# Packed attention and conditioning products held together, heads formed earlier, and an output projection over all columns at once, in a two-layer diffusion backbone

## The chip, the cores and the metric

The kernel runs on one core of one Trainium2 chip. The metric is the device time of one execution in microseconds (us). The engines are PE (TensorE, matrix products; PEld is its weight load), DVE (VectorE), ACT (ScalarE), POOL (GpSimd) and SP (SyncE, which here only issues transfers). Each engine works through its own list of instructions in order.

## The reference

Two layers over 256 context tokens and 256 latent tokens of width 1024. Each layer is an adaptive RMS norm, one input projection into three head groups (differential attention, multi-head latent attention, a two-directional gated recurrence), one output projection with a gated residual, and then the same around a squared-ReLU MLP. The shifts, scales and gates come from a conditioning vector and `w_mod`. Cut to what matters here:

```python
for l in range(2):
    mod = split(silu(c) @ w_mod[l] + b_mod[l], 6)          # 6 x 1024 columns, for latent and for context
    pl, pc = project(ada_norm(x, ...)), project(ada_norm(xc, ...))
    # differential attention (6 heads): softmax of two score sets, P0 - lam * P1, times v
    o_da  = diff_attn_core(pl['da_q'], k_da, v_da, lam)
    # latent attention (6 heads): scores of q_nope and q_rope against k_nope and k_rope, softmax, times v
    o_mla = mla_core(pl['q_nope'], pl['q_rope'], kn_all, kr_all, v_all)
    y = concat([da_post(o_da), o_mla, hgrn2_out(...)])     # 1024 wide
    x = x + mod[2] * (y @ w_out[l])
    x = x + mod[5] * (square(relu(ada_norm(x) @ w_ff1[l])) @ w_ff2[l])
    # in layer 0 the context tokens go the same way
return rmsnorm(x, g_final)
```

## The kernel before, in words

Activations are kept with features on the partitions. A float32 product in the large projections is made of three products of two rounded parts (`mm3`, L139 to L142: high by high, low by high, high by low). Weights come in units of 128 x 1024 through four `raw` buffers; ACT copies a unit into its high part `wh` and DVE subtracts to get the low part `wl` (`wunit`, L135 and L136), or POOL does, for as many units as the list `low` holds.

The program is written as one stream. A scheduler puts it into an order for each engine, by the priority of the place in the stream and by when it holds operands to be there; instructions that depend on nothing of each other can so be pulled apart.

Attention walks over steps: a differential step and a latent step in turn, one query tile of 128 rows each, three pairs of heads, 48 steps in layer 0 (four query tiles) and 24 in layer 1 (two). Each step has a part A (scores on PE, L930 and L1225; maximum on DVE; exponential on ACT), two steps later a part B (transposes of the probabilities, L907, and a copy out to `PT` or `mPT`), and a latent step has, three steps later, a part C for itself and its differential mate: the products of the probabilities with the values (L1239). The latent step's product writes one half of the output's 128 partitions and its mate's the other (`tile_position`), two or four key tiles each. A latent head's query and key (`mla_head`) are made by nine products, two ACT copies, a DVE shuffle and three POOL operations (L1191 to L1193); it is formed while its predecessor's step `nq // 2` is at hand. The steps of the next differential pair are staged by six small transfers on SP's queue and six on POOL's (L888).

Between steps of layer 0 a filler (`mod_group`) makes 4096 of the conditioning columns: two groups, each of eight sets, one for each eighth of the input. A set loads two `raw` units (L389, 512 KB each) and makes four products with a stationary operand of 32 columns (L392), one for each quarter of the output's partitions.

At the end of a layer's attention stand `late` tasks, among them the last pair's norm (`da_post`: L956 and a chain of small DVE operations) and the turning of the results into `yh` and `yl` (`turn_y`: L898, L901, L967 to L974). The output projection `proj_out` takes 512 columns at a time: in layer 1, six input tiles in three units for each half, and two more input tiles beside the steps. Each finished column tile is added to the residual on DVE (`ev_res`, L1011), squared on ACT and summed on DVE (L266) for the next norm, whose inputs `mhh` and `mhl` (L306, L307) the MLP's first product reads.

Of the kernel before, what the change touches and what calls it, by code (L numbers as in the profile page):

```python
# [8 lines left out]
F32 = mybir.dt.float32  # L9
# [31 lines left out]
def net(ctx: ExitStack, tc, x, c, cx, c_ctx, w_mod, b_mod, g_mix, g_mlp, w_in, w_out, da_lambda, da_subln_g,  # L41
# [97 lines left out]
    def mm3(ps, lh, ll, rh, rl, start, stop):  # L139
        PE.matmul(ps, lh, rh, start=start, stop=False)  # L140
        PE.matmul(ps, lh, rl, start=False, stop=False)  # L141
        PE.matmul(ps, ll, rh, start=False, stop=stop)  # L142

# [237 lines left out]

    def mod_group(l, g):
        started.append(1)
        ps = psum("mm")
        for k in range(KT):
            for hf in range(2):
                raw = raw_tile()
                c0 = g * 2048 + hf * 1024
                nc.sync.dma_start(out=raw, in_=w_mod[l].rearrange("(p k) f -> p k f", k=KT)[:, k, c0:c0 + 1024])  # L389
                for q in range(2):  # L390
                    j = 2 * hf + q
                    PE.matmul(ps[32 * j:32 * j + 32, :], scm[:, k, :], raw[:, 512 * q:512 * q + 512],  # L392
                              start=(k == 0), stop=(k == KT - 1))
            yield
# [197 lines left out]
    def layer(l):  # L592
# [432 lines left out]


# [184 lines left out]
        def mla_step(p, h, qi, qt, res):  # L1211
# [21 lines left out]
            def C():  # L1233
                d = s.mate
                op = psum("sc")
                for j in range(nk):
                    js = slice(128 * j, 128 * j + 128)
                    for PT, v, c, r in ((d.PT, dav, 2 * p + 1 - h, 1 - h), (s.PT, mv, hd, h)):
                        PE.matmul(op[64 * r:64 * r + 64, 0:128], v[:, j, 64 * c:64 * c + 64], PT[:, js], start=(j == 0),  # L1239
                                  stop=(j == nk - 1), tile_position=(0, 64 * r))  # L1240
                for r, o in ((1 - h, d.res["o"]), (h, res["o"])):
                    S.copy(out=o[64 * r:64 * r + 64, q0:q0 + 128], in_=op[64 * r:64 * r + 64, 0:128])
# [4 lines left out]
        def mla_steps():  # L1247
            order = [1, 0, 3, 2, 5, 4]
            for p in range(3):
                res = {}  # L1250
                for h in (1, 0):
                    for qi, qt in enumerate(qtiles):
                        s = mla_step(p, h, qi, qt, res)
                        n = 2 * p + 1 - h
                        if qi == nq // 2 and n < 5:
                            s.after = lambda n=n: heads.update({order[n + 1]: mla_head(order[n + 1], n + 1)})
# [17 lines left out]
        final = proj_out(0, 6 if last else KT, 512, True)  # L1274
# [21 lines left out]
        for _ in range(2):  # L1296
            step(final)
        if last:
            low.extend([G] * 3)
# [8 lines left out]
        with tc.tile_pool(name=f"mlp{l}", bufs=1) as fp:  # L1308
            fp.tile([128, 920], F32, name="gap")
# [135 lines left out]
```

## Time and profile before

| what | value |
|---|---|
| three runs: median (lowest to highest) | 1233.94 us (1233.19 to 1235.56) |
| the profiled execution: its time, its span | 1233.96 us, 1232.1 us |
| mean granted clock of PE | 0.993 |
| busy: PE, PEld, DVE, ACT, POOL | 1192.5, 964.9, 886.3, 581.8, 111.4 us |
| chain that ended last, by engine | PE 85%, DVE 8%, ACT 3%, POOL 1%, issue 1%, DMA 1% |
| moved by DMA | 170.93 MB, mean 139 GB/s |

The time of an execution is its span and a little around it. Busy time is the time in which an engine had at least one instruction at work; instructions on PE overlap, so that the mean length of one is more than the step from one to the next. The chain is followed back from the last instruction, at each step to what released it.

### The profile page before, as it was taken

Reading aid. Unit: us, or ns where it says so; the run is one execution under the profiler, and the core shown is the slowest. Engines: PE = TensorE matmul, PEld = TensorE weight load, DVE = VectorE, ACT = ScalarE, POOL = GpSimd, SP = SyncE. Lnnn points to the kernel's source line nnn. Section 1 sums busy time; section 2 is a strip of 40 time slices with the busy share of each in tenths; the row PEclk is TensorE's granted clock in tenths of the full one; section 3 lists DMA queues with packets and bytes.
Section 4 is the critical chain, followed back from the end, with each engine's and each line's share of the span. In section 5 each row is a group of like instructions: output and inputs, shape, how many; then the busy total and the mean of one; then the engine's idle time right before and its main releaser. Section 6 shows DMA issues by size and latency. Waiting matters only on the chain.

```text
span 1232.1 us, 21466 instructions
## 1 busy us (share of the span) xinstructions
PE 1192.5 (97%) x8318; PEld 964.9 (78%) x8318; DVE 886.3 (72%) x1786; ACT 581.8 (47%) x1114; POOL 111.4 (9%) x156
## 2 busy tenths in 40 slices
PE   6999999999999999999999999999998998999997
PEld 4677888855568777878787877787986678999997
DVE  4676587767676998765778675896788868765864
ACT  3534444576664553211233332554347874644653
POOL 2200000222200100000000000230003421000000
PEclk9999999999999999999999999999999998999999
DMA  9632223456543346555555555143314404555562
GB/s 325 191 85 57 69 58 100 120 155 196 184 168 103 103 136 194 189 165 162 177 156 156 170 170 151 55 122 92 93 54 131 127 18 135 176 186 178 184 186 69
DMA packets 138199, 170.93 MB, mean 139 GB/s; under 512 B 10883, under 2 KB 116033, under 8 KB 138097
## 3 DMA queue, kind: packets, MB, share of 16 engines
q1 hardware_dynamic: 134816, 164.08, 44.1%
q0 software_dynamic: 2704, 4.94, 1.7%
q8 instruction: 66, 1.08, 0.4%
q10 hardware_dynamic: 576, 0.53, 0.1%
q14 instruction: 37, 0.30, 0.1%
HBM read 160.21 MB, written 1.05 MB: 131 GB/s over the span
## 4 chain that ended last, share of the span: by engine, by line
PE 85%; DVE 8%; ACT 3%; POOL 1%; issue 1%; DMA 1%; SPq 0%; POOLq 0%; ACTq 0%; DVEq 0%
PE mm L140 21%; PE mm L142 21%; PE mm L141 20%; PE sc L1239 3%; PE sc L1225 2%; PE mm L392 2%; PE tp L907 2%; PE mm L218 2%; PE mm L219 2%; PE mm L220 2%; DVE wl L136 1%; PE sc L797 1%; PE mm L930 1%; PE sc L768 1%; PE sc L691 1%
## 5 line engine op out<-in xcount | busy, mean ns | idle before, releaser
L135 ACT CAST wh<-raw 128x1024 fp32r<-128x1024 f32 (+2 forms) x204 | 210.7, 1034 | 278.3 <-PE mm L141 199.6
L136 DVE TENSOR_TENSOR wl<-raw,wh 128x1024 fp32r<-128x1024 f32 (+2 forms) x201 | 242.6, 1209 | 108.8 <-ACT wh L135 106.3
L140 PE MATMUL mm<-mhh,wh 128*128 128x512 f32 (+1 forms) x512 | 173.0, 338 | 0.9 <-DVE fz L336 0.9
L140 PE MATMUL mm<-fa,wh 128*128 128x512 f32 (+1 forms) x512 | 172.5, 337 | 0.0
L141 PE MATMUL mm<-fb,wh 128*128 128x512 f32 (+1 forms) x512 | 171.9, 336 | 0.0
L142 PE MATMUL mm<-fa,wl 128*128 128x512 f32 (+1 forms) x512 | 171.9, 336 | 0.0
L142 PE MATMUL mm<-mhh,wl 128*128 128x512 f32 (+1 forms) x512 | 171.4, 336 | 0.4 <-DVE wl L136 0.4
L141 PE MATMUL mm<-mhl,wh 128*128 128x512 f32 (+1 forms) x512 | 171.7, 335 | 0.0
L426 DVE SCALAR_TENSOR_TENSOR room<-raw,scm,room 128x1024 f32<-128x1024 f32 x84 | 106.4, 1287 | 57.1 <-DMA raw<-in_w_mod_dram 57.1
L140 PE MATMUL mm<-hh,wh 128*128 128x512 f32 (+1 forms) x336 | 126.5, 381 | 4.6 <-ACT hh L351 3.3
L141 PE MATMUL mm<-hl,wh 128*128 128x512 f32 (+1 forms) x336 | 127.0, 378 | 2.3 <-DVE hl L352 2.3
L142 PE MATMUL mm<-hh,wl 128*128 128x512 f32 (+1 forms) x336 | 126.6, 377 | 1.1 <-DVE wl L136 1.1
L140 PEld LDWEIGHTS mm<-mhh,wh 128*128 128x128 f32 x512 | 96.3, 188 | 14.1 <-ACT wh L135 1.7
L140 PEld LDWEIGHTS mm<-fa,wh 128*128 128x128 f32 x512 | 97.0, 190 | 12.4 <-ACT wh L135 1.7
L142 PEld LDWEIGHTS mm<-fa,wl 128*128 128x128 f32 x512 | 97.1, 190 | 10.1
L141 PEld LDWEIGHTS mm<-fb,wh 128*128 128x128 f32 x512 | 97.2, 190 | 9.9
L142 PEld LDWEIGHTS mm<-mhh,wl 128*128 128x128 f32 x512 | 96.3, 188 | 11.0 <-DVE wl L136 0.8
L141 PEld LDWEIGHTS mm<-mhl,wh 128*128 128x128 f32 x512 | 96.3, 188 | 9.6
L140 PEld LDWEIGHTS mm<-hh,wh 128*128 128x128 f32 x336 | 63.4, 190 | 15.7 <-ACT hh L351 4.1
L141 PEld LDWEIGHTS mm<-hl,wh 128*128 128x128 f32 x336 | 64.2, 191 | 13.8 <-DVE hl L352 4.0
L142 PEld LDWEIGHTS mm<-hh,wl 128*128 128x128 f32 x336 | 64.1, 191 | 13.2 <-DVE wl L136 2.0
L347 POOL TENSOR_TENSOR nt<-nt,bc 128x256 f32<-128x256 f32 x24 | 27.0, 1131 | 483.6 <-ACT bc L326 436.1
(333 smaller groups left out, 2189.6 us busy)
## 6 DMA issues: line engine op xcount, KB each, us to landing
raw<-in_w_ff_dram SPq DMA_DIRECT2D x128, 512.0 KB, 3.8
raw<-in_w_mod_dram SPq DMA_DIRECT2D x80, 512.0 KB, 3.8
raw<-in_w_in_dram SPq DMA_DIRECT2D x42, 512.0 KB, 3.8
mraw<-in_w_mod_dram SPq DMA_DIRECT2D x32, 256.0 KB, 6.1
raw<-in_w_out_dram SPq DMA_DIRECT2D x10, 512.0 KB, 3.8
raw<-in_w_in_dram SPq DMA_DIRECT2D x16, 256.0 KB, 5.3
raw<-in_w_in_dram SPq DMA_DIRECT2D x8, 384.0 KB, 3.2
K<-dah POOLq DMA_DIRECT2D x48, 64.0 KB, 2.4
```

Of the source, the lines that this page charges most:

```text
L135: S.copy(out=wh, in_=raw)
L136: (low.pop() if low else V).tensor_sub(out=wl, in0=raw, in1=wh.bitcast(F32))
L140: PE.matmul(ps, lh, rh, start=start, stop=False)
L141: PE.matmul(ps, lh, rl, start=False, stop=False)
L142: PE.matmul(ps, ll, rh, start=False, stop=stop)
L218: PE.matmul(ps, a, wh[:, k, 0:w], start=st, stop=False)
L219: PE.matmul(ps, a, wl[:, k, 0:w], start=False, stop=False)
L220: PE.matmul(ps, b, wh[:, k, 0:w], start=False, stop=sp)
L347: G.tensor_mul(out=ts, in0=ts, in1=self.bc[:, a - T0:b - T0])
L392: PE.matmul(ps[32 * j:32 * j + 32, :], scm[:, k, :], raw[:, 512 * q:512 * q + 512], start=(k == 0), stop=(k == KT - 1))
L426: V.scalar_tensor_tensor(out=acc[r], in0=raw, scalar=scm[:, k, r:r + 1], in1=acc[r], op0=ALU.mult, op1=ALU.add)
L1239: PE.matmul(op[64 * r:64 * r + 64, 0:128], v[:, j, 64 * c:64 * c + 64], PT[:, js], start=(j == 0), stop=(j == nk - 1), tile_position=(0, 6 ...
```

## The change

It has six parts. First, `in_line` ties instructions in the order of a list, without a wait. Part C of a latent step ties its products, the latent one ahead of its mate's for each key tile, and gives them a high priority. Second, `mod_group` does the same with the four products of a set, and loads a set one call of the filler ahead of its products. Third, in layer 1 a head is formed at its predecessor's first step. Fourth, in layer 1 the last output projection takes one input tile and all 1024 columns at a time (`proj_wide`), in four PSUM tiles of two column tiles each; four input tiles of six go ahead of the `late` tasks (before: the first four input tiles for half of the columns). Fifth, `low` holds two units then, where it held three. Sixth, the tile `gap` is left out in layer 1.

```diff
     def mm3(ps, lh, ll, rh, rl, start, stop):
-        PE.matmul(ps, lh, rh, start=start, stop=False)
+        first = PE.matmul(ps, lh, rh, start=start, stop=False)
         PE.matmul(ps, lh, rl, start=False, stop=False)
         PE.matmul(ps, ll, rh, start=False, stop=stop)
+        return first
...
+    def in_line(instrs):
+
+        for a, b in zip(instrs, instrs[1:]):
+            tc.add_manual_dep(b.ins, a.ins.name, mybir.DependencyInfo(mybir.DependencyClass.NoSync,
+                                                                     mybir.DependencyReason.DATA), reason="in line")
+
     def mod_group(l, g):
         started.append(1)
         ps = psum("mm")
+
+        def load(k):
+            raws = [raw_tile() for _ in range(2)]
+            for hf in range(2):
+                c0 = g * 2048 + hf * 1024
+                nc.sync.dma_start(out=raws[hf], in_=w_mod[l].rearrange("(p k) f -> p k f", k=KT)[:, k, c0:c0 + 1024])
+            return raws
+
+        raws = load(0)
+        yield
         for k in range(KT):
-            for hf in range(2):
-                raw = raw_tile()
-                c0 = g * 2048 + hf * 1024
-                nc.sync.dma_start(out=raw, in_=w_mod[l].rearrange("(p k) f -> p k f", k=KT)[:, k, c0:c0 + 1024])
-                for q in range(2):
-                    j = 2 * hf + q
-                    PE.matmul(ps[32 * j:32 * j + 32, :], scm[:, k, :], raw[:, 512 * q:512 * q + 512],
-                              start=(k == 0), stop=(k == KT - 1))
+            now, raws = raws, load(k + 1) if k < KT - 1 else None
+            with tc.high_priority(1000):
+                in_line([PE.matmul(ps[32 * j:32 * j + 32, :], scm[:, k, :], now[j // 2][:, 512 * (j % 2):512 * (j % 2) + 512],
+                                   start=(k == 0), stop=(k == KT - 1)) for j in (2, 3, 0, 1)])
             yield
...
+        def proj_wide(ks):
+
+
+            pss = [psum("mm") for _ in range(4)]
+            ev = ev_res(16, 0, True)
+            for n, k in enumerate(ks):
+                wh, wl = wunit(w_out[l], 0, (k,), [(0, DM)])
+                yh, yl = (ydst[x][:, k, T0q:] for x in "hl")
+                for i in range(KT):
+                    ps, cs = pss[i // 2][:, 256 * (i % 2):256 * (i % 2) + 256], slice(128 * i, 128 * i + 128)
+                    first = mm3(ps, wh[:, 0, cs], wl[:, 0, cs], yh, yl, n == 0 and i % 2 == 0,
+                                n == len(ks) - 1 and i % 2 == 1)
+                    if n == 0 and i % 2:
+                        in_line([clear, first])
+                    clear = first
+                    if n == len(ks) - 1 and i % 2:
+                        ev(i - 1, pss[i // 2][:, 0:256])
+                        ev(i, ps)
+                yield
...
-                for j in range(nk):
-                    js = slice(128 * j, 128 * j + 128)
-                    for PT, v, c, r in ((d.PT, dav, 2 * p + 1 - h, 1 - h), (s.PT, mv, hd, h)):
-                        PE.matmul(op[64 * r:64 * r + 64, 0:128], v[:, j, 64 * c:64 * c + 64], PT[:, js], start=(j == 0),
-                                  stop=(j == nk - 1), tile_position=(0, 64 * r))
+                with tc.high_priority(1000):
+                    in_line([PE.matmul(op[64 * r:64 * r + 64, 0:128], v[:, j, 64 * c:64 * c + 64], PT[:, 128 * j:128 * j + 128],
+                                       start=(j == 0), stop=(j == nk - 1), tile_position=(0, 64 * r))
+                             for j in range(nk) for PT, v, c, r in ((s.PT, mv, hd, h), (d.PT, dav, 2 * p + 1 - h, 1 - h))])
...
-                        if qi == nq // 2 and n < 5:
+                        if qi == (0 if last else nq // 2) and n < 5:
...
-        final = proj_out(0, 6 if last else KT, 512, True)
+        final = proj_wide((0, 1, 3, 4, 5, 2)) if last else proj_out(0, KT, 512, True)
...
-        for _ in range(2):
+        for _ in range(4 if last else 2):
             step(final)
         if last:
-            low.extend([G] * 3)
+            low.extend([G] * 2)
...
-            fp.tile([128, 920], F32, name="gap")
+            if not last:
+                fp.tile([128, 920], F32, name="gap")
```

The order that the scheduler makes of it, at three places. The changed kernel's lines have other numbers: L1239 becomes L1270, L392 becomes L405, L907 becomes L920, L930 becomes L943, L1225 becomes L1258, L970 to L974 become L983 to L987, L1011 becomes L1024, and L266 and L307 become L267 and L308.

PE, some ten steps into layer 0's attention, before (`PT` are a differential step's probabilities, `mPT` a latent step's):

```order
L930 MATMUL mm<-K_2489,Q_2488 128x256 x2
L1239 MATMUL sc<-PT,dav 64x128
L392 MATMUL mm<-raw,scm 32x512
L907 MATMUL tp<-ident,P_2628 128x128 x2
L1239 MATMUL sc<-mPT,mv 64x128
L1239 MATMUL sc<-PT,dav 64x128
L1239 MATMUL sc<-mPT,mv 64x128
L1239 MATMUL sc<-PT,dav 64x128
L1239 MATMUL sc<-mPT,mv 64x128
L1239 MATMUL sc<-PT,dav 64x128
L1239 MATMUL sc<-mPT,mv 64x128
L392 MATMUL mm<-raw,scm 32x512
```

and at about the same place now:

```order
L141 MATMUL mm<-ckl,ukh 64x512
L1270 MATMUL sc<-mPT,mv 64x128
L1270 MATMUL sc<-PT,dav 64x128
L1270 MATMUL sc<-mPT,mv 64x128
L1270 MATMUL sc<-PT,dav 64x128
L405 MATMUL mm<-raw,scm 32x512 x4
L920 MATMUL tp<-ident,P_2627 128x128 x2
L920 MATMUL tp<-ident,mP 128x128 x2
L1258 MATMUL sc<-mk_2635,mq 128x512
```

A step's products and a set's four products stand together now, where one product of a step stood alone, with conditioning products before and after the rest. Over all of layer 0 the 64 conditioning products stand in 27 pieces before and 19 now (one row of eight counts as two), the attention products of 24 steps in 34 runs before and 25 now; in layer 1 those of 12 steps in 22 before and 12 now.

ACT, at the end of layer 1's attention, before (`oda` and `om` are the two kinds of attention's results):

```order
L1242 COPY oda<-sc 64x128
L1242 COPY om<-sc 64x128
L953 ACTIVATE P<-oda 128x256
L135 CAST wh<-raw 128x1024 x2
L970 CAST yh<-om 128x256
L292 CAST mhh<-modT_122 128x8x2
L973 ACTIVATE yh<-oda,vT_91 128x256
```

and now:

```order
L1274 COPY oda<-sc 64x128
L1274 COPY om<-sc 64x128
L966 ACTIVATE P<-oda 128x256
L135 CAST wh<-raw 128x1024 x4
L983 CAST yh<-om 128x256
L293 CAST mhh<-modT_122 128x8x2
L986 ACTIVATE yh<-oda,vT_91 128x256
```

Four weight casts stand ahead of the latent result's `yh` now, two before; the fourth is that of the MLP's first unit. On PE, 26 projection products stood before between the last sums of squares (L956) and the last transposes (L901, four in a row), and 72 stand there now (L969 and L914).

DVE, from the first residual addition of the tail on, before:

```order
L1011 SCALAR_TENSOR_TENSOR xT<-mm,modT_122,xT 128x256 x4
L136 TENSOR_TENSOR wl<-raw,wh 128x1024
L266 TENSOR_TENSOR nsq<-nsq 128x256
L307 SCALAR_TENSOR_TENSOR mhl<-xT,Gm_124,mhh 128x256
```

and now:

```order
L1024 SCALAR_TENSOR_TENSOR xT<-mm,modT_122,xT 128x256 x4
L267 TENSOR_TENSOR nsq<-nsq 128x256
L1024 SCALAR_TENSOR_TENSOR xT<-mm,modT_122,xT 128x256
L267 TENSOR_TENSOR nsq<-nsq 128x256
L1024 SCALAR_TENSOR_TENSOR xT<-mm,modT_122,xT 128x256
L267 TENSOR_TENSOR nsq<-nsq 128x256
L1024 SCALAR_TENSOR_TENSOR xT<-mm,modT_122,xT 128x256
L267 TENSOR_TENSOR nsq<-nsq 128x256
L1024 SCALAR_TENSOR_TENSOR xT<-mm,modT_122,xT 128x256
L308 SCALAR_TENSOR_TENSOR mhl<-xT,Gm_124,mhh 128x256
```

The first input of the norm (`mhl`) stood behind four additions, a weight subtraction and a sum; now it stands behind all eight additions and four sums.

## Rows read from the trace of the kernel before

**Rows 1.** The page: span, and busy us of PE with its share of the span.

```profile
span 1232.1 us, 21466 instructions
...
PE 1192.5 (97%) x8318; PEld 964.9 (78%) x8318; DVE 886.3 (72%) x1786; ACT 581.8 (47%) x1114; POOL 111.4 (9%) x156
```

**Rows 2.** Stretches: us; busy us (instructions) of PE, PEld, DVE, ACT, POOL; granted clock; DMA.

```profile
252.00:368.00 116.00, 115.86 (x754) 65.67 (x753) 81.93 (x230) 75.29 (x222) 22.43 (x39) 1.00 0.60 183
943.50:990.00 46.50, 41.72 (x280) 28.66 (x278) 39.53 (x95) 40.17 (x103) 22.89 (x39) 1.00 0.39 109
990.00:1013.67 23.67, 23.67 (x189) 17.29 (x188) 15.49 (x47) 17.20 (x47) 4.56 (x4) 1.00 0.08 24
1013.67:1022.00 8.33, 4.08 (x34) 3.87 (x34) 7.08 (x17) 2.39 (x3) 4.72 (x2) 0.86 0.22 65
1022.00:1026.60 4.60, 4.60 (x22) 4.60 (x23) 1.61 (x5) 0.83 (x3) 0.00 (x0) 0.51 0.39 114
1035.90:1047.80 11.90, 11.80 (x97) 11.48 (x97) 11.07 (x30) 7.23 (x13) 0.00 (x0) 1.00 0.60 181
```

**Rows 3.** The chain in layer 0's attention: start us, us, what.

```profile
252.28 0.99 PE mm L392 x8
...
261.06 0.97 PE mm L392 x2
```

**Rows 4.** PE in order of time, layer 0: start us, us, engine, line, operation, tiles.

```profile
260.62 0.43 PE L1239 MATMUL sc<-PT,dav 128*64 128x128 f32 x2
260.99 1.04 PE L392 MATMUL mm<-raw,scm 128*32 128x512 f32 x2
...
262.33 0.32 PE L1239 MATMUL sc<-mPT,mv 128*64 128x128 f32 x1
...
263.35 1.04 PE L392 MATMUL mm<-raw,scm 128*32 128x512 f32 x2
```

**Rows 5.** The loads of the conditioning weights (L389).

```profile
DMA to landing us min/median/max: 3.4/4.6/6.7
```

**Rows 6.** Waits of PE in layer 1's attention (total, times, longest), and PE's rows.

```profile
PE sc L1225 <- POOL mq L1193: 4.4, 5, 1.5
...
945.73 1.98 PE L1225 MATMUL sc<-mk,mq 96*128 96x512 f32 x4 [0.88 <-POOL mq L1193]
...
963.62 0.28 PE L142 MATMUL mm<-cqh,uql 128*96 128x256 f32 x1
...
968.36 1.12 PE L1225 MATMUL sc<-mk,mq 96*128 96x512 f32 x2 [0.46 <-POOL mq L1193]
```

**Rows 7.** The tail of layer 1's attention in order of time, all engines.

```profile
1013.67 0.61 PE L956 MATMUL tp<-halves,P 128*128 128x2 f32 x4
...
1014.54 1.05 ACT L135 CAST wh<-raw 128x1024 fp32r<-128x1024 f32 x1 [0.92 <-PE mm L141]
...
1015.40 0.16 DVE L235 TENSOR_TENSOR rs_t<-rs_t,rs_m 128x4 f32<-128x4 f32 x1
...
1015.67 2.38 POOL L136 TENSOR_TENSOR wl<-raw,wh 128x1024 fp32r<-128x1024 f32 x1 [5.60 <-ACT wh L135]
...
1015.79 2.28 DVE L234 SCALAR_TENSOR_TENSOR rs_t<-rs 128x4 f32<-128x4 f32 x1
...
1021.20 0.42 DVE L967 TENSOR_TENSOR om<-tp,om 128x256 f32<-128x256 f32 x1
...
1021.96 0.66 PE L901 MATMUL tp<-ident,P 128*128 128x128 f32 x2 [4.25 <-DVE P L898]
```

**Rows 8.** DVE behind it, in order of time.

```profile
1026.50 1.66 DVE L1011 SCALAR_TENSOR_TENSOR xT<-mm,modT,xT 128x256 f32<-128x256 f32 x4 [2.36 <-PE mm L142]
1028.40 1.23 DVE L136 TENSOR_TENSOR wl<-raw,wh 128x1024 fp32r<-128x1024 f32 x1 [0.24 <-ACT wh L135]
1029.55 0.42 DVE L266 TENSOR_TENSOR nsq<-nsq 128x256 f32<-128x256 f32 x1
1029.89 0.48 DVE L307 SCALAR_TENSOR_TENSOR mhl<-xT,Gm,mhh 128x256 fp32r<-128x256 f32 x1
```

## The prediction

> **What bounds the kernel now.** I read the page first: TensorE (PE) is busy for 1192.5 of 1232.1 us [rows 1], so a gain has to come from less PE work where PE never waits, or from fewer waits where it does. The table of stretches tells these apart [rows 2]. Layer 0's attention (252 to 368) has PE busy for 115.86 of 116.00 us, with VectorE (DVE) at 81.93 and ScalarE (ACT) at 75.29: there PE's own work is the bound. Layer 1's attention has two halves. From 943.5 to 990 PE is busy for 41.72 of 46.50 us, ACT for 40.17 and DVE for 39.53: three engines that take turns. From 990 to 1013.67 PE is full and ACT stands at 17.20 of 23.67. Then comes the tail: PE 4.08 of 8.33 us, and after it 4.60 us at a granted clock of 0.51, the lower of the two levels.
>
> **Layer 0: the conditioning products (L392).** On the chain a run of eight records (four products, one for each quarter of the output partitions) takes 0.99 us, a run of two records (one product) 0.97 [rows 3]. Four in a row thus cost what one costs; a run that is broken pays for each piece. Counted in the order, 64 products stand in 27 pieces before and 19 after (thirteen of four, three of three, three of one). Eight pieces fewer at 0.98 us: **-7.8 us**. The Trainium skill, "TensorE: Matmul & The Clock Gate", section "Measured speedup vs the span model", gives three column tiles a speedup of 2.38 and four row tiles 3.07. By that (an estimate from the page) a run of four would cost 1.26 us, a run of three 1.22, the new order 23.0 us against 26.5, and the gain would be 3.5 us instead of 7.8, the whole 1225.0. The trace shows 0.99 against 0.97, so I go by the trace.
>
> **Layer 0: the attention products (L1239).** They run in pairs too, one in each half of the output. A lone product holds PE from 260.62 to 260.99, that is 0.37 us; the seven that were left run from 262.33 to 263.35, 1.02 us, as long as four whole pairs [rows 4]. So each split costs 0.37 us. Layer 0 has 34 runs for 24 steps before and 25 after: nine fewer, **-3.3 us**.
>
> **Layer 0: what may take the place.** The conditioning products now go as soon as their loads are there, and stand in bursts: ten times the next set comes only some 3 to 4 us of PE work after the one before (an estimate, from the instructions between them at what such instructions take in layer 0). A set's two buffers come free when the set two places back has ended, so its loads have 6 to 8 us. Alone a load lands 3.4 to 6.7 us after its issue, 4.6 at the median [rows 5], and the second of a set is issued later than the first. PE executes in order, so a late load stops everything behind it. Lower end: no wait, as the trace of before has none in this stretch. Upper end: 0.8 us at each of those ten sets (6.7 plus 1.0 for the set two places back, less 6.9). I take the middle, 0.4 us at ten sets: **+4.0 us**. Layer 0 gives -7.1. The extra call of the filler and the later end of the second group (its transposes move behind the loop) cost nothing: layer 0's output projection follows at once and PE has work there; without that cover it would be a microsecond.
>
> **Layer 1: the heads.** PE waited 4.4 us in five places for the last of three GpSimd (POOL) operations that finish a head's query, 0.88 of it for the first head, which is formed where it was [rows 6]. From a head's last product at 963.62 to the first score that reads it 4.7 us pass. In the new order the other heads are complete 5 us of PE work or more ahead. So up to -3.5 us. On POOL's queue a head's operations now stand behind one staging transfer that waits for PE, and on ACT and DVE a copy and a shuffle come a step earlier; whatever they delay lies in this half.
>
> **Layer 1: the attention products.** 22 runs before, 12 after: four splits fewer ahead of 990, six behind it. The first half could lose 3.5 + 1.5 = 5.0 us and come to 41.5; but ACT has 40.17 us of work there, which would be 97% busy. Lower end of the gain: none (ACT and DVE set the pace); upper: 5.0. I take ACT at 93%, as it is 86% now and the waits for POOL are gone: 43.2, so **-3.3**. The second half is PE's own: 6 x 0.37 = **-2.2**.
>
> **Layer 1: the tail, the wide projection.** Before, 26 projection products stood between the last head's sums of squares (1013.67) and the transposes that end its chain; PE ran out and waited 4.25 us, then ran 22 records in 4.60 us where 0.12 us each would have been 2.6 [rows 7, 2]. Now 72 stand there, 8.6 us of cover. The chain in question is some dozen DVE operations at 0.2 us (0.16 and the step to the next), twice held up for 2.2 us while POOL subtracted weights (2.38 us); of three such subtractions two remain, and one of DVE's own (1.23) joins. Even so the chain ends about 7 us in. So **-4.25** and **-2.0** go. What is late next: both transposes now stand behind all 72, and behind them the MLA half's multiply (0.42), then on ACT a weight cast (1.05) that waits for PE and stands ahead of yh, then a DVE subtraction of 1.23 ahead of yl. From the last of the 72 to the first product with yl I count 2.8 us, with 1.0 us of PE work in it: **+1.75**.
>
> The bigger cost: all eight column tiles end together. Before, four residual additions, their squares and the norm's inputs were made while PE had the second half of the projection. Now DVE has in one row: 8 additions at 0.41, 7 sums at 0.34, 8 norm inputs at 0.39, 4 weight subtractions at 1.15 (from one start to the next), some 13 small operations at 0.2 [rows 8, 7]: 16.1 us, starting 2.2 us ahead of the projection's end. PE's part of it took 11.9 us before [rows 2]; it now ends when DVE's list does, at 13.9, and 2.0 later for what stands behind: 15.9. **+4.0**. Two products more lie ahead of the tail, -0.2. The tail as a whole: **-0.7**. A gain of 6 us is thus given back in the norm. Lower end -6.4 (POOL never collides, DVE keeps up), upper +4 (below). The new shape of the projection's weights (512 KB a unit as before) and the missing gap tile move no byte more.
>
> **Sum** against the profiled execution, 1233.96 us, of which the span is 1232.1 (the median of the runs is 1233.94): -7.1 - 3.3 - 2.2 - 0.7 = -13.3, so 1220.7.
>
> **Rivals.** (a) *All of the gain*: no wait for loads, no pace by ACT, the tail whole: -7.8 - 3.3 - 5.0 - 2.2 - 6.4 = -24.7, 1209.3. Against it: ACT at 97%, DVE's list. (b) *ACT and DVE set the pace* of the denser PE order: layer 1's first half keeps its 46.5 us, the second gains 1, layer 0 half of its 7.1, the tail 0.7: 1228.7. For it: 40.17 and 39.53 of 46.50. The Trainium skill, "TensorEngine Tiling (Array Packing)", section "PSUM Bottleneck", says that a faster TensorE can leave the PSUM copies as the bottleneck; layer 0's 82 of 116 us speak against it there, layer 1's row for it. (c) *The tail turns against the change*: the new gaps let the clock fall as the old one did (+2.0) and POOL's two subtractions fall on the norm's chain or the yl (+2.3): tail +4, 1225.4. For it: a gap of 2 us is expected at the start of the MLP. (d) *Slower: late loads stop PE in layer 0.* Each of 16 sets waits for its second load. From 1.1 us a set the whole gain of 17.3 (all but the 4.0 taken) is gone, from 1.24 the kernel is measurably slower; at 1.4 it takes 1239. For it: loads up to 6.7 us and sets 3 us apart, and six staging transfers of SyncE's queue between the loads, each time ahead of four or more loads. Against: PE waited for no load in all of this stretch before, with the same 16 MB. (e) *Nothing happens*: the order that the scheduler makes could break the groups again. The order shows that it does not in 13 of 16 sets, so 0.05 for a gain that other waits eat.
>
> **How the numbers follow.** Forecast 0.56, (a) 0.08, (b) 0.15, of which 0.02 within 0.2% (2.5 us, about what a measurement tells), (c) 0.09, (e) 0.05, (d) 0.07. Faster 0.86, same 0.07, slower 0.07. The range 1213 to 1230 leaves out (d), (e) and a part of (a), some 0.18; the forecast's own is 1215 to 1226.
>
> **What would show it.** Right: the conditioning products in some 19 pieces of 0.98 us; layer 0's attention 5 to 9 us shorter; no wait for POOL's query in layer 1; no gap of 4 us and no low clock at 1018; instead PE waits for DVE in the first weights of layer 1's MLP. Wrong: PE waits for loads of the conditioning weights that sum to over 8 us, ACT above 95% in layer 1, or a tail whose clock still falls.

## The result, and the profile after

The changed kernel takes 1220.41 us at the median of four runs (1214.33 to 1223.76), beside 1233.57 us for the kernel before on the same chip: the ratio is 0.9881, with a 95% interval from 0.9859 to 0.9904. A second set of runs (below) gave 1218.80 us and 0.9888. The prediction was 1220.7.

The page of the changed kernel, the lines that answer to [rows 1]:

```profile
span 1220.3 us, 21457 instructions
...
PE 1178.4 (97%) x8318; PEld 960.0 (79%) x8318; DVE 878.9 (72%) x1787; ACT 581.1 (48%) x1114; POOL 108.7 (9%) x155
```

PE works 14.1 us less and is still busy for 97% of the span: what was taken away is PE's own work. The table of stretches of the same execution, with the columns of [rows 2], by landmarks of the program: from layer 0's first score to the MLP's first product; from layer 1's first latent score to the product at which 990 us stood before, and on to the last sums of squares; then to the MLP's first product, and the first 97 instructions of PE from there.

```profile
247.00:400.30 153.30, 149.02 (x951) 96.97 (x950) 108.76 (x282) 95.64 (x270) 24.35 (x42) 0.99 0.53 165
943.07:982.57 39.50, 37.47 (x276) 27.58 (x276) 35.21 (x91) 36.05 (x94) 20.30 (x36) 1.00 0.46 128
982.57:1004.20 21.63, 21.31 (x192) 16.45 (x191) 16.08 (x51) 18.58 (x52) 2.70 (x3) 1.00 0.09 26
1004.20:1021.52 17.32, 15.96 (x129) 15.43 (x129) 8.57 (x28) 7.68 (x13) 4.80 (x2) 1.00 0.40 122
1021.52:1037.37 15.85, 13.86 (x100) 13.08 (x99) 14.18 (x39) 8.81 (x17) 0.00 (x0) 0.89 0.37 110
```

and the same stretches of the kernel before:

```profile
244.40:403.40 159.00, 158.44 (x951) 99.47 (x950) 109.13 (x282) 96.39 (x270) 24.31 (x42) 1.00 0.52 159
945.73:990.33 44.60, 40.70 (x276) 28.11 (x276) 37.70 (x93) 38.29 (x99) 20.74 (x36) 1.00 0.41 113
990.33:1013.67 23.34, 23.34 (x189) 17.28 (x188) 15.49 (x47) 16.87 (x46) 4.56 (x4) 1.00 0.08 24
1013.67:1035.88 22.21, 17.96 (x132) 17.64 (x131) 16.98 (x37) 9.16 (x17) 4.72 (x2) 0.85 0.32 93
1035.88:1047.94 12.06, 11.96 (x98) 11.64 (x98) 11.23 (x32) 7.26 (x14) 0.00 (x0) 1.00 0.60 178
```

So layer 0's attention with its projection lost 5.7 us, layer 1's attention 5.1 and 1.7, the way from there to the MLP 4.9; the MLP's opening gave 3.8 back. From layer 0's end to layer 1's first latent score 0.4 us were added, and 2.6 ahead of layer 0's first score, where the two kernels do the same work (see the last section). Behind the opening another 1.3 us went, which nothing in the prediction foresaw.

### The profile page after: what moved, and what is told of

It reads as the page before. It is cut to its first block, busy times and chain, and to the rows that moved or that the text cites. A ratio compares the mean times of both kernels' runs of the same rounds, so it can differ in the third digit from the quotient of the medians.

```text
span 1220.3 us, 21457 instructions
## 1 busy us (share of the span) xinstructions
PE 1178.4 (97%) x8318; PEld 960.0 (79%) x8318; DVE 878.9 (72%) x1787; ACT 581.1 (48%) x1114; POOL 108.7 (9%) x155
## 3 DMA queue, kind: packets, MB, share of 16 engines
HBM read 160.21 MB, written 1.05 MB: 132 GB/s over the span
## 4 chain that ended last, share of the span: by engine, by line
PE 81%; DVE 9%; ACT 4%; DMA 3%; issue 1%; POOL 1%; SPq 0%; DVEq 0%; ACTq 0%; POOLq 0%
PE mm L142 20%; PE mm L140 20%; PE mm L141 20%; PE sc L1270 2%; DMA raw<-in_w_mod_dram 2%; PE tp L920 2%; PE mm L219 2%; PE mm L220 2%; PE mm L221 2%; PE sc L1258 2%; PE mm L405 2%; DVE wl L136 1%; PE sc L810 1%; PE sc L781 1%; PE sc L704 1%
## 5 line engine op out<-in xcount | busy, mean ns | idle before, releaser
L348 POOL TENSOR_TENSOR nt<-nt,bc 128x256 f32<-128x256 f32 x24 | 26.5, 1111 | 489.3 <-ACT bc L327 439.9
```

What stands on the lines that cost most here:

```text
L348: G.tensor_mul(out=ts, in0=ts, in1=self.bc[:, a - T0:b - T0])
```

## The experiments

All of them in one table. The three stretches are read from one profile each: layer 0 from the first score of its attention to the MLP's first product, layer 1 from the first latent score to the last sums of squares, the tail from there to the end. (The expectations measure layer 0's attention to its last sums of squares. Work crosses that point when the order changes, so the table goes on to the MLP.)

| kernel | median us | ratio to before, 95% interval | layer 0 | layer 1 | tail |
|---|---|---|---|---|---|
| before | 1233.4 to 1235.0 | 1 | 159.0 | 67.9 | 218.5 |
| changed | 1220.41 | 0.9881 [0.9859, 0.9904] | 153.3 | 61.1 | 216.1 |
| changed, again | 1218.80 | 0.9888 [0.9871, 0.9905] | 151.8 | 61.0 | 215.1 |
| att_only | 1238.27 | 1.0028 [1.0015, 1.0041] | 162.1 | 68.5 | 218.2 |
| mod_only | 1228.52 | 0.9952 [0.9935, 0.9970] | 151.1 | 68.0 | 219.2 |
| heads_only | 1235.04 | 1.0009 [0.9993, 1.0024] | 159.0 | 66.8 | 218.5 |
| no_heads | 1225.05 | 0.9924 [0.9902, 0.9946] | 150.3 | 69.7 | 213.8 |
| no_wide | 1220.70 | 0.9889 [0.9867, 0.9910] | 150.7 | 60.4 | 219.1 |
| untied | 1222.50 | 0.9903 [0.9881, 0.9925] | 157.4 | 60.8 | 216.3 |
| no_ahead | 1220.68 | 0.9889 [0.9870, 0.9908] | 151.9 | 60.8 | 215.5 |
| two_ahead | 1218.85 | 0.9877 [0.9859, 0.9896] | 152.5 | 60.8 | 214.4 |
| split_early | 1218.32 | 0.9868 [0.9846, 0.9889] | 154.7 | 61.1 | 214.2 |
| low4 | 1221.30 | 0.9893 [0.9874, 0.9911] | 152.2 | 61.1 | 219.5 |
| best | 1215.01 | 0.9851 [0.9828, 0.9874] | 152.4 | 60.8 | 212.7 |

**The changed kernel again.** No edit.

> The changed kernel once more, unchanged, for a second profile and a closer median. Theory: its runs of 1214 to 1224 us differ by what one execution meets, in layer 0 (a wait of 1.8 us for a conditioning load and the fall of the clock behind it, in no other profile with that order) and in the norm of the tail (a fall of the clock at 1024 us). Another profile then shows layer 0's attention at 110 to 113 us (from the first score to the last sums of squares) and the tail, from the last sums of squares to the end, at 213.8 to 216.1; the median within 1218 to 1222. Rival (the waits belong to this order of the kernel): the same wait of 1.8 us and the same fall at the same place, 113 and 216 again.

The median of 1218.80 lies where it was expected. On the cause of the spread the theory was half wrong: the wait is there again, 1.7 us ahead of the same set, and so is the fall of the clock in the MLP's opening (3.4 us in both profiles); only the fall behind the wait is not. PE in order of time in this second profile, and its waits in layer 0 (total, times, longest):

```profile
328.94 1.02 PE L1258 MATMUL sc<-mk,mq 96*128 96x512 f32 x2
331.67 1.06 PE L405 MATMUL mm<-raw,scm 128*32 128x512 f32 x6 [1.70 <-DMA raw<-in_w_mod_dram]
...
PE mm L405 <- DMA raw<-in_w_mod_dram: 2.0, 2, 1.7
PE sc L1270 <- DVE mPT L922: 0.7, 2, 0.5
PE mm L140 <- ACT wh L135: 0.6, 1, 0.6
PE mm L140 <- ACT P L949: 0.4, 1, 0.4
PE sc L1258 <- ACT mP L1261: 0.4, 1, 0.4
```

The loads behind it were issued when the set two places back had ended, and the later one landed 7.3 us after its issue. In the six profiles with this order of layer 0 (changed, again, no_heads, no_wide, split_early, low4) this load took 5.1 to 9.0 us and PE waited for it between nothing and 3.4. So the wait belongs to the order, its length to the execution.

**Layer 0: the attention products alone, the conditioning products alone.** att_only and mod_only put one part of the change onto the kernel before:

```diff
 # att_only: C() only
...
+                with tc.high_priority(1000):
+                    in_line([PE.matmul(op[64 * r:64 * r + 64, 0:128], ... tile_position=(0, 64 * r))
+                             for j in range(nk) for PT, v, c, r in ((s.PT, ...), (d.PT, ...))])
 # mod_only: mod_group() only, as in the changed kernel
```

> The kernel before with one part of the change: the attention products tied in order. In the order the runs of attention products fall from 34 to 24 in layer 0 and from 22 to 12 in layer 1, but the conditioning products, untied, now stand in 32 pieces, before in 27. Theory (each piece costs, 0.98 us for a conditioning piece and 0.37 us for an attention run): layer 0 +4.9 - 3.7 = +1.2 us, layer 1's attention (first latent score to the last sums of squares, 67.9 us before) up to -3.7 us, the tail as before; in all -2.5 us, about 1231. Rival (the pieces cost nothing, since other engines set the pace in both layers): within 1 us of before, layer 0's attention unchanged.

> The kernel before with one part of the change: the conditioning products tied in fours, and their loads a call ahead. Pieces fall from 27 to 16, the runs of layer 0's attention products rise from 34 to 38. Theory: -10.8 + 1.5 = -9.3 us, less the waits for loads (2.1 us in the changed kernel's profile): about -7 us, 1226.5, all of it in layer 0's attention. Rival (the bursts of loads give it back): PE waits 6 us or more for loads and the kernel is within 2 us of before.

att_only is slower, against its theory and against its rival. The theory misses in both layers: layer 0 is 3.1 us longer where it had 1.2, and layer 1's attention 0.5 longer where it had up to 3.7 less (see the part on layer 1). What makes it slower than before is layer 0, and a count explains most of that: tied and with high priority, the attention products break up the conditioning products. PE's busy time in the conditioning products and in the attention products of layer 0 (the stretch, then PE and PEld of that line alone), before:

```profile
244.40:403.40 159.00, 28.47 (x128) 3.96 (x128) 1.00 0.52 159
244.40:403.40 159.00, 25.23 (x288) 17.03 (x288) 1.00 0.52 159
```

in att_only:

```profile
244.20:406.30 162.10, 33.67 (x128) 4.61 (x128) 1.00 0.51 156
244.20:406.30 162.10, 21.03 (x288) 15.26 (x288) 1.00 0.51 156
```

and in the second profile of the changed kernel, with all of PE in the first row:

```profile
245.10:396.90 151.80, 147.44 (x951) 96.41 (x950) 108.75 (x282) 95.60 (x269) 24.20 (x41) 1.00 0.53 167
245.10:396.90 151.80, 19.96 (x128) 3.02 (x128) 1.00 0.53 167
245.10:396.90 151.80, 21.45 (x288) 15.41 (x288) 1.00 0.53 167
```

| layer 0 | before | att_only | mod_only | untied | changed, again |
|---|---|---|---|---|---|
| conditioning: pieces, us | 27, 28.47 | 32, 33.67 | 16, 16.63 | 29, 30.58 | 19, 19.96 |
| attention products: runs, us | 34, 25.23 | 24, 21.03 | 38, 26.79 | 24, 21.03 | 25, 21.45 |
| PE idle (stretch less busy) | 0.56 | 2.07 | 1.49 | 1.34 | 4.36 |

A piece takes 28.47 / 27 = 1.05 us in every column but one (1.04 in mod_only), of which the last 0.07 lies under the next instruction: 0.98 on the path, as predicted. A run that is split off costs (25.23 - 21.03) / 10 = 0.42, less the same 0.07: 0.35, where the prediction had 0.37. By these prices att_only should lose 4.9 - 3.5 + 1.5 (idle) = 2.9 us in layer 0; it loses 3.1. mod_only gains 10.8 - 1.4 - 0.9 = 8.5; measured 7.9. As a whole mod_only is 5.9 us faster for the 7 that its theory gave, and PE waits 0.3 us for a load, not the rival's 6. The idle time in these sums is measured, so that they test the two prices alone.

**Layer 0: tie or earlier load?** untied takes the ties and the priority from the conditioning products of the changed kernel, no_ahead loads each set in its own call, two_ahead loads two sets ahead:

```diff
 # untied
-            with tc.high_priority(1000):
-                in_line([PE.matmul(...) for j in (2, 3, 0, 1)])
+            for j in range(4):
+                PE.matmul(...)
 # no_ahead
-        raws = load(0)
-        yield
         for k in range(KT):
-            now, raws = raws, load(k + 1) if k < KT - 1 else None
+            now = load(k)
 # two_ahead
-            raws = [raw_tile() for _ in range(2)]
+            raws = [wp.tile([128, 1024], F32R, tag=t, name=t, bufs=3).bitcast(F32) if k % 3 == 2 else raw_tile()
+                    for t in ("wh", "wl")]
...
+            if k < KT - 2:
+                loaded.append(load(k + 2))
```

> The changed kernel with the four products of a conditioning set neither tied nor given priority, their loads still a call ahead. In the order the pieces rise from 19 to 29, the runs of layer 0's attention products fall from 25 to 24. Theory (a piece costs 0.98 us): layer 0's conditioning products +9.8 us (18.7 before the edit), fewer waits for loads (-1 to -2), layer 0's attention 118 to 120 us after 110 to 113, the whole +7 to +8, about 1227. Rival (the earlier loads bring the gain, not the ties): 111 to 113 us, the whole within 2 us of the changed kernel.

> The changed kernel with the sets tied, but each set's loads in its own call of the filler, not one call ahead. In the order 19 pieces, as many as in the changed kernel. Theory (a load is issued when its buffer comes free, wherever it stands in the program, so the call ahead is worth little): layer 0's attention 110 to 114 us, waits for loads 1 to 4 us, the whole within 2 us of the changed kernel. Rival (the call ahead keeps PE from waiting): waits for loads of 6 us or more, layer 0's attention 117 or more, the whole +5.

> The changed kernel with the loads of the conditioning weights two sets ahead, not one: every third set is loaded into a pair of the weights' wh and wl buffers, which layer 0's attention leaves unused. The order also joins more: 17 pieces (a row of eight counts as two), before the edit 19. Theory (late loads cost the changed kernel 2.1 us and a fall of the clock, some 3 us in its profile, 0.7 in two others): no wait for a load, layer 0's attention at 108 to 110 us, the whole -1 to -3 us. Rival (the loads are rarely late and other waits take their place): layer 0's attention 110 to 111, within 1 us.

In untied the ten pieces more cost what the theory says (30.58 - 19.96 = 10.6 us of PE's busy time), yet layer 0 is only 5.6 us longer than in the changed kernel's second profile, and the whole some 2 to 4: of PE's 4.36 us of idle time 3.0 are gone, among them both waits for loads, since a PE that is slower meets its loads and copies ready. Some 2 us more do not appear in the length: 0.7 of the pieces' time lies under the next instructions, 0.4 the attention products give back, and the rest was not followed. The whole is nearer the rival's bound than the theory's. In no_ahead nothing changes beyond the noise: the call ahead is worth nothing that these runs can tell, and the gain of this part is that of the ties with their priority (no run took those two apart). In two_ahead no wait for a load is left, but layer 0 is no shorter: PE waits 1.5 us for DVE's copies to `mPT`, 2.1 in all for ACT's exponentials of the differential steps, and others. The rival holds there. The Trainium skill, "TensorEngine Tiling (Array Packing)", section "PSUM Bottleneck", says that tiles run side by side speed up TensorE and not the copies out of PSUM, which may become the bottleneck. Of these waits the 1.5 us for `mPT` are for such copies, 1% of the stretch's 152 us.

**Layer 1: which part shortens it?** no_heads is the changed kernel with the heads formed where they were, heads_only the kernel before with only that part:

```diff
-                        if qi == nq // 2 and n < 5:
+                        if qi == (0 if last else nq // 2) and n < 5:   # heads_only; no_heads the other way round
```

> The changed kernel with the heads formed where they were (at the predecessor's step nq // 2). Layer 1's attention from the first latent score to the last sums of squares took 67.9 us before and 61.1 in the changed kernel. Theory (3.5 us of waits for the query's POOL operations come back): 64 to 65 us in that stretch, the whole +3 us, about 1223.5. Rival (the packing alone made layer 1 shorter, ACT and DVE set the rest): 61 to 62 us, the whole within 1 us of the changed kernel.

> The kernel before with one part of the change: in layer 1 a head is formed at its predecessor's first step. Layer 1's attention took 67.9 us before, 68.5 with the packing alone, 69.7 with all but the heads, 60.4 and 61.1 with both. Theory (the query's chain over ACT, DVE and POOL sets the pace of the first half, so that the packing alone only makes PE wait longer): the heads alone take off the 4.4 us of waits, 63 to 64 us, and the packing is worth its 2.5 to 3.5 us only behind them; the whole about -4 us, 1230. Rival 1 (both parts are needed, each alone is worth nothing): 67 to 68 us. Rival 2 (the heads do all of it, the packing nothing): 60 to 62 us, the whole -7.

Both at once give 6.8 us, and neither alone gives more than 1.1; no expectation had this right but the rival that both are needed, and it with 67 to 68 us. PE's waits for the query of a latent head in the run with the packing alone:

```profile
PE sc L1231 <- POOL mq L1199: 6.6, 6, 1.4
```

with the heads alone:

```profile
PE sc L1225 <- POOL mq L1193: 0.8, 1, 0.8
```

and in the changed kernel, with what comes in their place:

```profile
PE sc L1270 <- ACT mPT L922: 1.2, 3, 0.7
PE sc L1258 <- POOL mq L1226: 0.8, 1, 0.8
PE tp L920 <- DVE P L953: 0.7, 1, 0.7
```

| layer 1's attention | before | att_only | heads_only | changed |
|---|---|---|---|---|
| attention products: runs, us | 22, 17.19 | 12, 13.13 | 24, 17.83 | 12, 13.13 |
| PE idle (stretch less busy) | 3.91 | 6.95 | 2.13 | 2.35 |
| length | 67.94 | 68.45 | 66.80 | 61.13 |

The packing alone saves PE 4.06 us in these products; then PE waits 3.04 us longer, mostly for the same POOL operations ([rows 6] had 4.4 us of that wait), and 1.5 us more of its other work fall into the stretch: the query's chain, not PE, sets when the next score can start. no_heads shows the same wait (6.7 us, six times); its 69.7 us also hold 3.4 us at the lower clock, which att_only's 68.5 do not. The heads alone take 3.5 us of that wait away, but PE's idle time falls by 1.8 only, since new waits for DVE and ACT come up (0.9 us at most each), and the attention products, in two runs more, take 0.6 us of it back. With both, the products give 4.06 us, the waits 1.56, and PE's other work 1.2 (three products of a head fall ahead of the stretch, and the transposes stand in 20 rows where they stood in 23; this was not followed further).

**The tail.** no_wide is the changed kernel with the old end, split_early turns the latent half behind the first unit and finishes column tiles 0 to 3 ahead of 4 to 7, low4 gives POOL four subtractions:

```diff
 # no_wide
-        final = proj_wide((0, 1, 3, 4, 5, 2)) if last else proj_out(0, KT, 512, True)
+        final = proj_out(0, 6 if last else KT, 512, True)
...
-        for _ in range(4 if last else 2):
+        for _ in range(2):
-            low.extend([G] * 2)
+            low.extend([G] * 3)
...
-            if not last:
-                fp.tile([128, 920], F32, name="gap")
+            fp.tile([128, 920], F32, name="gap")
 # split_early
         for i in range(4 if last else 2):
             step(final)
+            if last and i == 0:
+                late.pop(0)()                     # the latent half's turn_y
...
+            for cols in (range(4), range(4, 8)):  # the last two units, half of the column tiles at a time
+                for j in range(2):
+                    part(len(ks) - 2 + j, us[j], cols)
 # low4
-            low.extend([G] * 2)
+            low.extend([G] * 4)
```

> The changed kernel with the old end of layer 1's attention (projection by halves of 512 columns, two steps ahead of the late tasks, three weight subtractions on POOL, the gap tile). From the last sums of squares to the end: 218.4 us before, 216.1 in the changed kernel's profile. Theory (a gap of 4 us and a fall of the clock come back, the norm's long list on DVE goes): 218 to 219, the whole +2 to +3 us, about 1223. Rival (the wide projection costs as much in the norm as it saves): 216 to 217, the whole within 1 us of the changed kernel.

> The changed kernel with two edits in the tail: the latent half of the last pair is turned behind the first of the four units, not behind all four, and the last two units of the projection are worked through by halves of the column tiles (tiles 0 to 3 of both, then 4 to 7). The tail took 216.1 us in the changed kernel and 213.8 in the same tail of the run without the heads. Theory (PE waits 1.36 us for the turning and yl, and 2.0 us in the norm for DVE's list, which now starts 1.5 us earlier): 211 to 213, and no fall of the clock there; the whole -2 to -3 us against the changed kernel. Rival (DVE's list sets the end whatever the order): 213 to 216, within 1 us of the changed kernel.

> The changed kernel with four weight subtractions on POOL in the tail, where it has two: those of the MLP's first two units leave DVE's list. Theory (DVE's list sets the pace of the norm): 2.3 us less on it, the tail 1 to 2 us shorter than the changed kernel's 215.1 and 216.1. Rival (a subtraction on POOL holds up the DVE operations beside it, 2.2 us each as it did before the change): DVE gives back what it gains, the tail 215 to 219.

no_wide has the old tail back, 219.1 us, as the theory said; but its median is that of the changed kernel. Its profile has 150.7 us in layer 0, where the changed kernel's two have 153.3 and 151.8, and medians of 4 to 6 runs leave 2 to 3 us on either side. That the new end pays is shown by the profiles of the tail (213.8 to 216.3 in the six profiles that have it as the change made it, 218.2 to 219.2 in the five without it), not by the times. How much of it is the wide projection's is less: up to the end of the MLP's opening the two profiles of the changed kernel are 1.1 and 1.2 us shorter than before, and the other 1.3 and 2.1 us lie behind it, in products that the projection does not touch (see the last section). no_wide takes the projection, the subtractions and the gap tile back together, and no run took them apart. split_early is 1 to 2 us below the changed kernel's tail; its expected 211 to 213 came only in the run named best. What it gains is the way to the MLP's first product, 16.5 us for 17.3; the opening, with a fall of the clock in it, takes as long as the changed kernel's.

low4 is where the rival holds, with a tail of 219.5 us even beyond its 219. DVE, then POOL, then PE of it in order of time:

```profile
1011.89 2.37 DVE L984 TENSOR_TENSOR yl<-om,yh 128x256 fp32r<-128x256 f32 x1 [0.42 <-ACT yh L983]
...
1019.24 1.66 DVE L1024 SCALAR_TENSOR_TENSOR xT<-mm,modT,xT 128x256 f32<-128x256 f32 x4 [3.57 <-PE mm L142]
1020.91 1.34 DVE L267 TENSOR_TENSOR nsq<-nsq 128x256 f32<-128x256 f32 x1
...
1011.63 2.35 POOL L136 TENSOR_TENSOR wl<-raw,wh 128x1024 fp32r<-128x1024 f32 x1 [0.48 <-ACT wh L135]
1019.58 2.39 POOL L136 TENSOR_TENSOR wl<-raw,wh 128x1024 fp32r<-128x1024 f32 x1 [5.59 <-ACT wh L135]
...
1014.32 0.46 PE L141 MATMUL mm<-yl,wh 128*128 128x256 f32 x1 [1.67 <-DVE yl L984]
```

The third subtraction ends at 1013.98, and `yl`, 0.42 us of work, ends 0.3 us behind it, 2 us late; PE waits 1.67 us for it, and the granted clock falls to 0.50 behind that wait, from 1014.5 to 1017.9. The four residual additions that run beside the fourth, with one input from PSUM, take their usual 1.66 us, while the sum of squares behind them, with both inputs from SBUF, takes 1.34 us where the next takes 0.41. The Trainium skill, "SBUF — State Buffer", section "Who interferes with whom", has the rule: a DVE instruction with two SBUF inputs contends with a GpSimd instruction that reads SBUF, and one with at most one SBUF input, outside certain performance modes, does not. These rows agree.

**Both improvements.** best is two_ahead with split_early's tail.

> The changed kernel with both improvements so far: the conditioning loads two sets ahead (no wait for a load, but 1.5 us more for a step's copies) and the tail with the earlier turn and the split projection (214.2 us with a fall of the clock in it). Theory: 1 to 3 us under the changed kernel, 1216 to 1218. Rival (what one engine gives another takes): within 1 us of it, 1218 to 1220.

It is the fastest kernel of the study: 1215.01 us, 1 us below its theory's range, a ratio of 0.9851 with an interval that still touches that of the changed kernel. Its tail of 212.7 us has no fall of the clock in the MLP's opening: the first 97 instructions take 14.20 us. Against the changed kernel's second profile (span 1215.0, best 1211.3) the tail gives 2.4 us and the time ahead of layer 0 3.0, which the edits don't touch; layer 0 gives nothing. So part of its lead may be the clock of the executions and not the edits.

## Why the prediction was right, step by step

The sum was -13.3 us. The measured differences of the profiles, and of which parts they are made:

| step | predicted | changed | changed, again |
|---|---|---|---|
| ahead of layer 0 | 0 | +2.6 | +0.7 |
| layer 0 | -7.1 | -5.7 | -7.2 |
| between | 0 | +0.4 | -0.4 |
| layer 1's attention | -5.5 | -6.8 | -6.9 |
| tail | -0.7 | -2.4 | -3.3 |
| span | -13.3 | -11.8 | -17.1 |

**Layer 0** came out as the prediction put it, and att_only and mod_only show its prices: 0.98 us a piece, 0.35 a run. By an estimate from the Trainium skill, "TensorE: Matmul & The Clock Gate", section "Measured speedup vs the span model", whose figure for four tiles is for tiles in rows, a run of four would have cost 1.26 us; no column of the table bears that out. The 3.5 us that the prediction drew from that estimate were no like for like: it set the new order at the estimate's prices against 26.5 us, which is the old order at the trace's price (27 pieces of 0.98). The +4.0 for late loads was right as a sum and wrong in its make-up: PE's idle time rose by 3.8, of which loads are 2.0, at two sets and not at ten, and waits for copies and exponentials the rest; that the two sums agree is luck. Rival (d), that late loads eat the gain, had one place where it is true; rival (b) had the waits for other engines right in kind, but at 1.8 us, not at half of the gain.

**Layer 1** was taken too small, and there a step of the argument failed. The prediction added the heads (-3.5) and the splits (-1.5) in the first half and then took ACT at 93% for the bound, 43.2 us for 46.5. It gave 5.1 us, where the upper bound was 5.0. ACT's 40.17 us had been counted from 943.5, 2.2 us ahead of the first score; between the landmarks it was 38.29, and 36.05 after, 91% of 39.50. Nor is it fixed: five of ACT's exponentials that ran in the first half now run in the second, where ACT is busy for 18.58 us after 16.87 and was not the bound. That the two parts are worth hardly anything alone the prediction did not say; it only follows from the runs. The second half lost 1.7 for 2.2.

**The tail.** The way to the MLP's first product lost 4.9 us, with -4.25 - 2.0 + 1.75 - 0.2 = -4.7 predicted. Its opening gave 3.8 back (12.06 to 15.85), with +4.0 predicted; DVE is busy for 14.18 of 15.85 us, and PE waits 2.0 us for its residual additions. A fall of the clock has a part in that, the prediction's rival (c): in no_heads, where it does not fall, the same instructions take 14.58 us with DVE at 14.15:

```profile
1027.35:1041.93 14.58, 12.58 (x99) 11.75 (x98) 14.15 (x39) 8.79 (x17) 0.00 (x0) 1.00 0.40 119
```

two_ahead, without a fall there too, takes 14.58 as well. So 2.5 us are DVE's list and 1.3 the clock. The +4.0 thus came out by luck: it was put down to DVE's list and what stands behind it, which are worth 2.5 (the items of that list add up to 16.0 us, not 16.1), and a fall of the clock that the sum did not hold made up most of the rest. A tail whose clock still falls was also a sign by which the prediction wanted to be judged wrong. It came in both profiles of the changed kernel, for 3.4 us in the MLP's opening, where the kernel before has 6.8 us of it ahead of the MLP. What made the tail better than predicted came behind the opening: there the changed kernel is 1.3 and 2.1 us shorter, to which the prediction gave no price. It says that the projection's weights and "the missing gap tile move no byte more"; whether the gap tile is the reason is not shown (last section).

That the median lies 0.3 us from the prediction is partly chance: layer 1 and the rest of the MLP gave some 3 us more than predicted, and the first profile lost about as much in and ahead of layer 0, where its clock is lower for longer (last section). The ratio's interval, -17.4 to -11.8 us of 1233.57, holds both.

## What to carry to other kernels

Count in how many pieces a group of products that run side by side stands in the order; pieces times the price of one predicted PE's busy time in layer 0 to within 0.8 us in four orders, and tying one group can break another (att_only). Where two things end a wait in turn, as PE's order and the query's chain in layer 1, take away both before judging either: alone, one gave 1.1 us and the other lost 0.5, and together they gave 6.8. And a faster PE waits more: a third of the 11 us that the ties saved in layer 0 came back as small waits, so reckon with it. Before moving work to POOL, see which DVE operations run beside it: those with two SBUF operands were held up here.

## What the runs showed of the hardware that was not expected

**The same products run at different speeds.** The same 1034 products and what stands between them in the second layer's MLP, PE busy throughout at full clock, in no_wide, which keeps the gap tile and the old projection:

```profile
1075.73:1199.68 123.95, 123.95 (x1036) 123.83 (x1035) 79.66 (x130) 62.01 (x91) 0.00 (x0) 1.00 0.55 175
```

in the changed kernel, without them, and in untied, which differs from it in layer 0 only:

```profile
1078.72:1200.95 122.23, 122.23 (x1037) 122.06 (x1035) 79.74 (x131) 62.24 (x91) 0.00 (x0) 1.00 0.57 177
...
1075.85:1198.97 123.12, 123.12 (x1037) 122.97 (x1035) 79.77 (x130) 62.05 (x91) 0.00 (x0) 1.00 0.56 176
```

All five profiles with the gap tile and the old projection have 123.95 us. Of the nine without them six have 122.2 to 122.3, two_ahead and low4 122.6, untied 123.1. So 0.8 to 1.7 us of 124 go with the new end of layer 1, and the changed kernel's second profile repeats its time (122.26). The gap tile shifts the buffers behind it, which would be a reason; but no run took it away alone, and low4 and untied, whose edits name no other tile, differ from the changed kernel too. The cause stays open.

**The clock falls in some executions and not in others at the same place.** In the changed kernel's first profile the granted clock is 0.50, the lower of the two levels, for 3.4 us behind the wait of 1.8 us in layer 0 (PE's row with that wait, then the two stretches), and for 10.3 us in the kernel's beginning:

```profile
333.75 1.06 PE L405 MATMUL mm<-raw,scm 128*32 128x512 f32 x6 [1.80 <-DMA raw<-in_w_mod_dram]
...
335.00:338.40 3.40, 3.40 (x19) 1.41 (x15) 0.00 (x0) 0.52 (x2) 0.00 (x0) 0.50 0.58 160
17.50:27.80 10.30, 7.94 (x58) 4.51 (x58) 4.88 (x12) 5.30 (x9) 1.67 (x2) 0.50 1.10 349
```

In its second profile the clock stays at full speed behind a wait of 1.7 us at the same place, and in two_ahead it does not fall in the beginning at all:

```profile
17.50:27.80 10.30, 7.63 (x94) 4.28 (x92) 4.88 (x12) 5.29 (x9) 1.68 (x2) 1.00 1.10 349
```

The first score of layer 0 comes at 242.0 to 247.0 us in the 14 profiles, and the time at the lower clock ahead of it goes with that: 242.0 to 242.9 us where there is none (untied, best, two_ahead), 244.2 to 245.1 with 3.4 or 6.8 us of it, 246.3 to 247.0 with 10.2 to 17.1. That spread of 5 us is about half of the 9.4 us by which the runs of the changed kernel differ.
